# A decoder trunk on one Trainium2 core: the order and the loads of its first projections rewritten

## The chip, the core and the metric

The kernel runs on one of the eight cores of a Trainium2 chip. A core has five engines that run their own instruction queues in order and meet only at semaphores: TensorE (PE, matrix products; its weight loads are listed as PEld), VectorE (DVE), ScalarE (ACT), GpSimd (POOL) and SyncE (SP, which here issues loads). Sixteen DMA engines move data between HBM and the on-chip memory; PE writes its results to PSUM, eight banks of 128 partitions by 512 floats.

The metric is the device time of one execution in microseconds, the median of several runs. Lower is better.

## What is computed

A two-layer decoder trunk on 256 tokens of width 2048, in float32. Layer A mixes by chunked spatial gating beside cross-attention into 256 memory tokens; layer B by latent attention beside the same cross-attention; a gated feed-forward with a short convolution follows each. The change concerns what both cross-attentions need first, the keys and values of the memory, and the norm and turning of the input x:

```python
def rmsnorm(x, g):
    x32 = x.astype(jnp.float32)
    y = x32 * lax.rsqrt(jnp.mean(x32 * x32, axis=-1, keepdims=True) + EPS)
    return (y * g.astype(jnp.float32)).astype(x.dtype)

def memory_attention(q_m, mem, g_mem, w_mem_kv):
    kv = rmsnorm(mem, g_mem) @ w_mem_kv          # (256 x 2048) @ (2048 x 1024)
    k, v = kv[..., :MEM_W], kv[..., MEM_W:]      # 4 heads of 128 each
    ...
    return softmax(q k^T / sqrt(128)) v

for l in range(2):
    h = rmsnorm(x, g_mix[l])
    ...
    mo = memory_attention(q_m, mem, g_mem[l], w_mem_kv[l])
    x = x + concat(main, mo) @ w_out[l]
    x = x + conv_ffn(rmsnorm(x, g_ffn[l]), ...)
```

## The kernel before

Activations stand with features on partitions and tokens along the free axis, in blocks of 128 features: 16 blocks for a width of 2048. Every float32 operand of a product is split in two parts: a rounded high part (type fp32r) and the low part that the rounding left. An activation's two parts lie side by side as 128 x 512 (256 tokens high, 256 low); a weight tile has `whi` and `wlo`.

A projection goes in chunks of 512 KB of weights: two blocks of 128 rows by 512 columns. `chunk` (L92) loads one (L98, issued by SP, into one of five `raw` buffers), lets ACT round it to `whi` (L122, one instruction for each block, with the gain folded in) and DVE form `wlo` (L123). There are three buffers each of `whi` and `wlo`. Two kinds of projection use it:

- `gemm_fm` (L158), features out on partitions. A chunk gives eight high products of 512 columns (L140) and eight low products of 256 (L144), into four PSUM banks; `mm_fm` (L135) alternates which kind goes first from chunk to chunk (its argument `turn`).
- `gemm_tm` (L184), tokens out on partitions. A chunk gives twelve products of 512 columns (L179, L180, L181) into two banks.

Both take `hooks`: functions that are called in the code after a given chunk's products.

`start` (L417) is the beginning of the kernel. It makes keys and values of the memory for both layers: for each layer a `gemm_fm` (keys) and a `gemm_tm` (values), eight chunks each, four projections in a row. Around them it prepares inputs by hooks:

- `token_load` (L380) loads a quarter of the memory (or of x) as two pieces of 128 tokens by 512 features, 256 KB each (L383).
- `token_transpose` (L385) turns four blocks by PE transposes against the identity, four for each PSUM bank (L390), and hands the bank to `put_mem`, where ACT copies the high part (L436) and DVE forms the low part (L437) of `memhl`, or to `put_x`, where the gain is applied (L231, L232) and x is copied (L442).
- `token_rstd` (L395) sums squares by ACT (L402, eight instructions for the memory, eight for x), then a short chain on DVE and ACT gives the reciprocal root (L241 to L246; its square root L242 needs an activation table load). `spread` (L407) turns it to the feature layout by two products with ones.
- `gains` (L301) loads gain vectors (L309), turns them (L313) and stores them as columns of `gT`; the first weights' rounding needs `g_mem`.

The memory's reciprocal root scales the keys in their eviction (`ek`, L470: ACT copies, DVE adds, GpSimd multiplies by `mrb`, L471) and the values in theirs (L474). The keys are read first by `memory_scores` (L485) in layer A.

The code is a recording: a scheduler orders each engine's instructions by its own estimate of times, from their data dependencies. Within a `manual_schedule` context the listed engines keep the order of the code. Before the change no part of `start` stands in one.

## Time and profile before

| | |
|---|---|
| median of 3 runs | 2126.27 us (2125.35 to 2126.89) |
| the profiled execution | 2125.63 us |
| its span, first to last instruction | 2123.9 us |
| PE busy | 2101.8 us (99%) |
| DVE, ACT, POOL busy | 1464.5, 1147.8, 319.6 us |
| HBM read | 387.88 MB |
| granted TensorE clock over the span | 0.999 |

How to read it: one execution was recorded by the hardware profiler; times are microseconds from the span's start. Matrix products are pipelined and the ends of their records are modelled, so the records overlap and busy time is not peak use; the distance from one product's start to the next is the better measure. A timeline merges neighbouring instructions of one engine, line and operation: it gives the first start, the time to the last end, and the count; in brackets, the engine's idle time before and what ended it. A window row gives, for PE, PEld, DVE, ACT and POOL, busy time and (in brackets) instructions, then the granted clock, the share of the 16 DMA engines and GB/s. A group's row gives line, engine, operation, output and input names, shapes, count, total busy time, mean duration in ns of one, and the idle time before.

### The profile page before, as it was taken

The numbers are of one execution on the slowest core, as the hardware profiler recorded it, in microseconds if no ns is written. First come the engines' busy times: TensorE is split into PE (matmuls) and PEld (weight loads), VectorE is DVE, ScalarE is ACT, GpSimd is POOL, SyncE is SP. The second block draws the span as 40 slices with busy tenths as digits, with TensorE's granted clock in tenths as the row PEclk, the third lists the DMA queues.
The fourth block names the chain that finished last, engine by engine and source line by source line (L and its number), as shares of the span: only waits on it lengthen the run. The fifth ranks groups of instructions, "written<-read, shape, count | busy, mean of one in ns | idle before, by whom it ended". The sixth has DMA issues, their size and how long they took to land.

```text
span 2123.9 us, 31119 instructions
## 1 busy us (share of the span) xinstructions
PE 2101.8 (99%) x11624; PEld 1828.7 (86%) x11624; DVE 1464.5 (69%) x2186; ACT 1147.8 (54%) x1773; POOL 319.6 (15%) x378
## 2 busy tenths in 40 slices
PE   8999999999999999999999999999999999999998
PEld 7888888888888888888888888888888888888886
DVE  6656667777656776567788676777764677646775
ACT  7654744556435555355546555456553555535554
POOL 0000123212001110011244111221110011100110
PEclk9999999999999999999999999999999999999999
DMA  8566565666566665666555533665666666666654
GB/s 277 177 204 183 155 194 187 188 190 191 189 192 183 197 187 191 188 189 189 188 183 168 161 115 122 188 188 176 190 191 195 189 188 190 193 193 189 188 188 149
DMA packets 207548, 392.01 MB, mean 185 GB/s; under 512 B 14302, under 2 KB 22820, under 8 KB 207268
## 3 DMA queue, kind: packets, MB, share of 16 engines
q1 hardware_dynamic: 207252, 389.50, 60.4%
q8 instruction: 91, 1.49, 0.3%
q14 instruction: 61, 0.50, 0.1%
q10 hardware_dynamic: 144, 0.52, 0.1%
HBM read 387.88 MB, written 2.10 MB: 184 GB/s over the span
## 4 chain that ended last, share of the span: by engine, by line
PE 98%; DVE 1%; ACT 0%; POOL 0%; DMA 0%; issue 0%; SPq 0%; DVEq 0%; ACTq 0%
PE ps L140 51%; PE ps L144 26%; PE ps L179 6%; PE ps L181 6%; PE ps L180 6%; PE ps L829 1%; PE ps L827 0%; PE ps L520 0%; PE ps L390 0%; DMA raw<-in_w_mem_kv 0%; PE ps L485 0%; PE ps L663 0%; DVE wlo L106 0%; PE ps L850 0%; PE ps L935 0%
## 5 line engine op out<-in xcount | busy, mean ns | idle before, releaser
L118 DVE TENSOR_TENSOR wlo<-raw,whi 128x1024 fp32r<-128x1024 f32 x660 | 817.9, 1240 | 494.1 <-ACT whi L117 490.1
L117 ACT ACTIVATE whi<-raw 128x1024 fp32r<-128x1024 f32 x660 | 697.7, 1057 | 640.8 <-PE ps L140 422.2
L140 PE MATMUL ps<-xhl,whi 128*128 128x512 f32 x3280 | 789.3, 391 | 1.6 <-ACT whi L122 1.6
L140 PEld LDWEIGHTS ps<-xhl,whi 128*128 128x128 f32 x3280 | 601.5, 188 | 117.1 <-ACT whi L122 1.8
L144 PEld LDWEIGHTS ps<-xhl,wlo 128*128 128x128 f32 x3280 | 423.3, 191 | 17.9 <-DVE wlo L106 0.7
L144 PE MATMUL ps<-xhl,wlo 128*128 128x256 f32 x3280 | 432.3, 283 | 0.2 <-DVE wlo L106 0.2
L568 POOL TENSOR_TENSOR a<-js,rbc 128x256 f32<-128x256 f32 x176 | 170.1, 978 | 1164.5 <-DVE js L221 1015.2
L140 PE MATMUL ps<-h,whi 128*128 128x512 f32 x704 | 168.6, 391 | 0.0
L140 PEld LDWEIGHTS ps<-h,whi 128*128 128x128 f32 x704 | 129.3, 188 | 25.0
L571 ACT ACTIVATE c<-a,cT 128x256 f32<-128x256 f32 x176 | 100.0, 592 | 77.1 <-POOL a L568 77.1
L219 ACT ACTIVATE cr<-ps 128x256 f32<-128x256 f32 x243 | 90.6, 379 | 92.0 <-PE ps L140 82.9
L180 PE MATMUL ps<-wlo,h 128*128 128x512 f32 x352 | 136.4, 389 | 0.0
L181 PE MATMUL ps<-whi,h 128*128 128x512 f32 x352 | 136.4, 389 | 0.0
L179 PE MATMUL ps<-whi,h 128*128 128x512 f32 x352 | 123.6, 389 | 0.0
L140 PE MATMUL ps<-mainhl,whi 128*128 128x512 f32 x512 | 122.7, 391 | 0.0
L221 DVE TENSOR_TENSOR js<-ps,cr 128x256 f32<-128x256 f32 x213 | 89.5, 421 | 44.7 <-ACT cr L219 24.6
L123 DVE SCALAR_TENSOR_TENSOR wlo<-raw,gT,whi 128x512 fp32r<-128x512 f32 x112 | 87.4, 819 | 32.8 <-ACT whi L122 31.7
L140 PEld LDWEIGHTS ps<-mainhl,whi 128*128 128x128 f32 x512 | 94.1, 188 | 18.2
L573 DVE SCALAR_TENSOR_TENSOR c<-a,cT,c 128x254 f32<-128x254 f32 x176 | 102.9, 586 | 1.6
L572 DVE SCALAR_TENSOR_TENSOR c<-a,cT,c 128x255 f32<-128x255 f32 x176 | 93.3, 550 | 13.4 <-ACT c L571 12.4
L122 ACT ACTIVATE whi<-raw,gT 128x512 fp32r<-128x512 f32 x112 | 74.8, 716 | 40.4 <-PE ps L140 16.7
L144 PEld LDWEIGHTS ps<-h,wlo 128*128 128x128 f32 x704 | 90.4, 191 | 3.5
(248 smaller groups left out, 1847.0 us busy)
## 6 DMA issues: line engine op xcount, KB each, us to landing
raw<-in_w_ffn_up SPq DMA_DIRECT2D x352, 512.0 KB
raw<-in_w_ffn_down SPq DMA_DIRECT2D x176, 512.0 KB
raw<-in_w_out SPq DMA_DIRECT2D x64, 512.0 KB
raw<-in_w_in_a SPq DMA_DIRECT2D x56, 512.0 KB
raw<-in_w_mem_kv SPq DMA_DIRECT2D x32, 512.0 KB
raw<-in_w_in_b SPq DMA_DIRECT2D x16, 512.0 KB
raw<-in_w_uq SPq DMA_DIRECT2D x12, 384.0 KB
raw<-in_w_kv_a SPq DMA_DIRECT2D x8, 512.0 KB
```

What stands on the lines that cost most here:

```text
L117: nc.scalar.activation(hi[:, :n], raw[:, :n], AF.Copy)
L118: nc.vector.tensor_tensor(lo[:, :n], raw[:, :n], hi[:, :n].bitcast(F32), ALU.subtract)
L140: mm(acc[:, :], wh, x, start=first, stop=last)
L144: mm(acc[:, S:], wl, x[:, :S], start=False, stop=False)
L179: mm(acc, xh, wh, start=first, stop=False)
L180: mm(acc, xh, wl, start=False, stop=False)
L181: mm(acc, xl, wh, start=False, stop=last)
L219: self.nc.scalar.activation(cr, acc[:, S:], AF.Copy)
L568: nc.gpsimd.tensor_tensor(a, self.join(acc), rb, ALU.mult)
L571: nc.scalar.activation(c, a, AF.Identity, scale=w(2), bias=w(3))
L572: nc.vector.scalar_tensor_tensor(c[:, 1:], a[:, : S - 1], w(1), c[:, 1:], ALU.mult, ALU.add)
L573: nc.vector.scalar_tensor_tensor(c[:, 2:], a[:, : S - 2], w(0), c[:, 2:], ALU.mult, ALU.add)
```

## The change

All of it lies in the helpers named above and in `start`:

- The memory's loads are cut differently: blocks 0 to 1, 2 to 3, 4 to 7, 8 to 11, 12 to 15. The first two pieces go out on SP with `g_mem` between them. The third pair follows before the projection; the last two are hooks after chunks 1 and 3.
- The first weights' load is issued by ACT, ahead of everything else there, and given to `chunk` ready made.
- The first projection (keys, layer 0) stands in `manual_schedule` for ACT, DVE, PE and SP. Blocks 0 to 3 are turned ahead of it, blocks 4 to 15 by hooks, two blocks (one PSUM bank, four transposes) after each of the chunks 0 to 5. `mm_fm` gets turn 0 for all its chunks: high products first.
- The memory's squares move from the first projection to the value projection of layer 0 (after chunks 0 and 1), the squares of x from one hook (chunk 4 of layer 1's keys) to four (chunk 6 of layer 1's keys, chunks 0 to 2 of its values); `token_rstd` keeps the sum and the root, with one reduction in place of two. The squares are kept in the order of the code.
- The keys of layer 0 are evicted unscaled (ACT, DVE), and `scale_keys` multiplies them in place on GpSimd once `mrb` is known.
- The loads and turns of x and the constants move between hooks as shown.

```diff
-    def chunk(self, src, nk, ncol, gains=None, twice=False, heads=None):
+    def chunk(self, src, nk, ncol, gains=None, twice=False, heads=None, raw=None):
         nc, n = self.nc, nk * ncol
-        raw = self.wp.tile([P, 1024], F32, tag="raw", name=self.uid("raw"), bufs=5)
+        loaded = raw is not None
+        if not loaded:
+            raw = self.wp.tile([P, 1024], F32, tag="raw", name=self.uid("raw"), bufs=5)
...
-        nc.sync.dma_start(out=view(raw), in_=src)
+        if not loaded:
+            nc.sync.dma_start(out=view(raw), in_=src)
...
-    def gemm_fm(self, src, kbs, nblk, rhs, evict, nk=2, gain=None, hooks={}):
+    def gemm_fm(self, src, kbs, nblk, rhs, evict, nk=2, gain=None, hooks={}, raw=None):
...
-            hi, lo = self.chunk(src(kbs[c], nk), nk, nblk * P, g)
+            hi, lo = self.chunk(src(kbs[c], nk), nk, nblk * P, g, raw=raw if c == 0 else None)
...
-            self.mm_fm(jobs, (c // nk) % 2)
+            self.mm_fm(jobs, (c // nk) % 2 if raw is None else 0)
...
-    def token_load(self, src, tok, h):
-        c = slice(h * 512, (h + 1) * 512)
+    def token_load(self, src, tok, k0, k1):
+        c = slice(k0 * P, k1 * P)
...
-    def token_transpose(self, tok, h, put):
-        for k in range(4 * h, 4 * h + 4, 2):
+    def token_transpose(self, tok, k0, k1, put):
+        for k in range(k0, k1, 2):
...
+    def token_squares(self, tok, part, j, pool):
+        for tb in range(2):
+            junk = self.tmp(pool, [P, 512], "junk", 2)
+            ins = self.nc.scalar.activation(
+                junk, tok[tb][:, j * 512 : (j + 1) * 512], AF.Square, accum_out=part[:, tb, j : j + 1]
+            )
+            self.tc.keep_in_program_order(ins)
+
+    def token_rstd(self, part, pool, rt):
         sums = self.tmp(pool, [P, 2], "sums", 1)
-        for tb in range(2):
-            part = self.tmp(pool, [P, 4], "part", 2)
-            for j in range(4):
...
+        self.nc.vector.tensor_reduce(sums, part, AX.X, ALU.add)
         self.rstd(rt, sums, D, self.cp, "rt")
...
+            def scale_keys():
+                self.spread(mrb, mrt)
+                for b in range(MH):
+                    nc.gpsimd.tensor_tensor(self.kT[0][:, b, :], self.kT[0][:, b, :], mrb, ALU.mult)
+
+            raw = self.wp.tile([P, 1024], F32, tag="raw", name=self.uid("raw"), bufs=5)
+            src = self.rows(t["w_mem_kv"][0], 0, MW)(0, 2)
+            nc.scalar.dma_start(out=raw.rearrange("p (k c) -> p k c", k=2), in_=src)
+            mload(0, 2)()
             self.gains(("g_mem",))
-            self.token_transpose(mtok, 0, put_mem)
+            mload(2, 4)()
+            first = {c: [mturn(2 * c + 4, 2 * c + 6)] for c in range(6)}
+            first[1].insert(0, mload(8, 12))
+            first[3].insert(0, mload(12, 16))
             hooks = [
+                first,
                 {
-                    0: [mem_piece(1)], 2: [mem_piece(2)], 4: [mem_piece(3)],
-                    5: [lambda: self.token_rstd(mtok, st, mrt), lambda: self.gains(("g_mix", "g_ffn", "g_kv"))],
-                    6: [self.masks],
-                    7: [lambda: self.spread(mrb, mrt)],
+                    0: [lambda: self.gains(("g_mix", "g_ffn", "g_kv")), xload(0, 4), msq(0), msq(1)], 1: [xload(4, 8), msq(2), msq(3)],
+                    2: [lambda: self.token_rstd(mpart, st, mrt), xload(8, 12)], 3: [xload(12, 16), xturn(0, 4)], 4: [self.masks],
+                    5: [scale_keys], 6: [lambda: self.gains(("g_v", "g_kv_lat", "g_q_lat"))],
                 },
+                {0: [xturn(4, 8)], 2: [xturn(8, 12)], 4: [xturn(12, 16)], 6: [xsq(0)]},
                 {
-                    0: [load(0), load(1)], 1: [load(2), load(3)], 3: [trans(0)], 5: [trans(1)],
-                    6: [lambda: self.gains(("g_v", "g_kv_lat", "g_q_lat"))],
+                    0: [xsq(1)], 1: [xsq(2)], 2: [xsq(3), lambda: self.conv_consts(0)], 3: [lambda: self.token_rstd(xpart, st, self.rt)],
+                    5: [lambda: self.spread(self.rb, self.rt), lambda: self.conv_consts(1)],
                 },
-                {0: [trans(2)], 2: [trans(3)], 4: [lambda: self.token_rstd(xtok, st, self.rt)]},
-                {1: [lambda: self.spread(self.rb, self.rt)], 2: [lambda: self.conv_consts(0)], 4: [lambda: self.conv_consts(1)]},
             ]
...
                 def ek(b, acc):
-                    nc.gpsimd.tensor_tensor(kT[:, b, :], self.join(acc), mrb, ALU.mult)
+                    if l == 0:
+                        self.join(acc, kT[:, b, :])
+                    else:
+                        nc.gpsimd.tensor_tensor(kT[:, b, :], self.join(acc), mrb, ALU.mult)
...
-                self.gemm_fm(self.rows(w, 0, MW), list(range(NB)), MH, m, ek, gain=g, hooks=hooks[2 * l])
+                ET = mybir.EngineType
+                with tc.manual_schedule(engines={ET.Activation, ET.DVE, ET.PE, ET.SP}) if l == 0 else nullcontext():
+                    if l == 0:
+                        mload(4, 8)()
+                        mturn(0, 2)()
+                        mturn(2, 4)()
+                    self.gemm_fm(
+                        self.rows(w, 0, MW), list(range(NB)), MH, m, ek, gain=g, hooks=hooks[2 * l], raw=raw if l == 0 else None
+                    )
```

Here `mload`, `mturn`, `xload`, `xturn`, `msq` and `xsq` wrap `token_load`, `token_transpose` and `token_squares` for the memory and for x. Lines below the edits stand 3 to 30 further down in the changed kernel: L122 becomes line 125, L140 line 143, L144 line 147, L179 to L181 lines 182 to 184, L390 line 393, L436 line 442.

More of the change, by code (lines that the diff above doesn't have):

```diff
@@ L442, in put_x @@
                 nc.scalar.activation(self.x[:, k : k + 2, :], acc.rearrange("p (k s) -> p k s", k=2), AF.Copy)
-            def mem_piece(h):
-                return lambda: (self.token_load(t["mem"][0], mtok, h), self.token_transpose(mtok, h, put_mem))
-            load = lambda h: lambda: self.token_load(t["x"][0], xtok, h)
-            trans = lambda h: lambda: self.token_transpose(xtok, h, put_x)
-            self.token_load(t["mem"][0], mtok, 0)
+            mload = lambda k0, k1: lambda: self.token_load(t["mem"][0], mtok, k0, k1)
@@ new lines, in start @@
+            mturn = lambda k0, k1: lambda: self.token_transpose(mtok, k0, k1, put_mem)
+            xload = lambda k0, k1: lambda: self.token_load(t["x"][0], xtok, k0, k1)
+            xturn = lambda k0, k1: lambda: self.token_transpose(xtok, k0, k1, put_x)
+            mpart = st.tile([P, 2, 4], F32, name="mpart")
+            xpart = st.tile([P, 2, 4], F32, name="xpart")
+            msq = lambda j: lambda: self.token_squares(mtok, mpart, j, st)
+            xsq = lambda j: lambda: self.token_squares(xtok, xpart, j, st)
```

5 lines of the change are left out of this document (removed).

## The prediction

> **What bounds the kernel now.** First the page: span, busy time, the chain that ended last.
>
> ```profile
> span 2123.9 us, 31119 instructions
> PE 2101.8 (99%) x11624; PEld 1828.7 (86%) x11624; DVE 1464.5 (69%) x2186; ACT 1147.8 (54%) x1773; POOL 319.6 (15%) x378
> ...
> PE 98%; DVE 1%; ACT 0%; POOL 0%; DMA 0%; issue 0%; SPq 0%; DVEq 0%; ACTq 0%
> ```
>
> PE (TensorE's matrix products) is busy for 99% of the span and holds 98% of the chain, so a change counts by the time in which it makes PE stand or run slowly, and by nothing else. Such time is named by the waits of PE over the whole span (waited for, us in total, times, longest):
>
> ```profile
> PE ps L313 <- DMA graw<-in_g_mem: 5.8, 1, 5.8
> PE ps L140 <- ACT whi L122: 2.8, 2, 1.6
> PE ps L140 <- DVE qhl L232: 1.6, 1, 1.6
> ```
>
> Only the first wait, and 1.2 of the second's 2.8 us, lie in the beginning that the change rewrites. So I read the timeline of its first microseconds (start, us from the first start to the last end, engine, line, operation, count, idle before):
>
> ```profile
> 5.81 0.28 PE L313 MATMUL ps<-ident,graw 32*128 32x32 f32 x1 [5.81 <-DMA graw<-in_g_mem]
> 6.02 1.97 PE L390 MATMUL ps<-ident,mtok 128*128 128x128 f32 x8
> ...
> 7.17 0.60 ACT L436 ACTIVATE memhl<-ps 128x512 fp32r<-128x512 f32 x1 [2.91 <-PE ps L390]
> ...
> 8.40 1.33 ACT L122 ACTIVATE whi<-raw,gT 128x512 fp32r<-128x512 f32 x2 [0.63 <-DMA raw<-in_w_mem_kv]
> ...
> 9.16 1.42 DVE L123 SCALAR_TENSOR_TENSOR wlo<-raw,gT,whi 128x512 fp32r<-128x512 f32 x2 [0.66 <-ACT whi L122]
> ...
> 9.18 2.07 PE L140 MATMUL ps<-memhl,whi 128*128 128x512 f32 x4 [1.19 <-ACT whi L122]
> ...
> 11.05 1.91 PE L390 MATMUL ps<-ident,mtok 128*128 128x128 f32 x8
> ...
> 12.61 1.64 PE L140 MATMUL ps<-memhl,whi 128*128 128x512 f32 x4
> 12.65 0.57 ACT L436 ACTIVATE memhl<-ps 128x512 fp32r<-128x512 f32 x1
> ...
> 13.13 1.32 ACT L122 ACTIVATE whi<-raw,gT 128x512 fp32r<-128x512 f32 x2
> ...
> 13.50 0.68 DVE L437 TENSOR_TENSOR memhl<-ps,memhl 128x512 fp32r<-128x512 f32 x1
> ...
> 14.09 1.60 PE L144 MATMUL ps<-memhl,wlo 128*128 128x256 f32 x12
> ```
>
> and of PE alone a little later:
>
> ```profile
> 24.27 1.04 PE L390 MATMUL ps<-ident,mtok 128*128 128x128 f32 x8
> 25.07 2.11 PE L140 MATMUL ps<-memhl,whi 128*128 128x512 f32 x8
> 27.02 2.08 PE L144 MATMUL ps<-memhl,wlo 128*128 128x256 f32 x16
> 28.93 2.01 PE L140 MATMUL ps<-memhl,whi 128*128 128x512 f32 x8
> 30.78 0.23 PE L313 MATMUL ps<-ident,graw 80*128 80x80 f32 x1
> ...
> 36.93 0.39 PE L179 MATMUL ps<-whi,memhl 128*128 128x512 f32 x1
> ```
>
> The step from one row's start to the next's start, divided by the count, is the pitch. Settled: high products (L140) (30.78 - 28.93) / 8 = 0.231 us, low products (L144) (28.93 - 27.02) / 16 = 0.119, transposes (L390) (25.07 - 24.27) / 8 = 0.100. Early it is twice that: four high products from 9.18 to 11.05 (0.47 each), eight transposes from 11.05 to 12.61 (0.195); at 14.09 the low products go at (1.60 - 0.28) / 11 = 0.12. So PE runs at half speed until about 13.6 us and at full speed after (the windows' clock column, below, says 1.00 throughout; the pitch decides). From 9.18 to 36.93 are 27.75 us; the stretch holds 64 high, 64 low products, 24 transposes and five small ones: 64 x 0.231 + 64 x 0.119 + 24 x 0.100 + 0.5 = 25.3. The 2.4 us over it are the slow phase. The first projection is therefore already full after 14 us: what the change can win lies before, and what it can lose is any hole that it cuts afterwards.
>
> **The change, part by part.** PE's work itself stays: the same 32 transposes of memory, products and spreads.
>
> *The written order* is the part that decides. In the first projection PE, ACT, DVE and SP keep the order in which the code stands. Chunk c's products are followed by its hook, the four transposes of two more blocks and their copy by ACT (L436 now, line 442 after), and only then comes the chunk call for c+1, with ACT's rounding of its weights (L122 now, 125 after). The built program has it so; ACT's queue from its start:
>
> ```
> L442 Activation memhl_81<-ps_121 128x2x256
> L125 Activation whi_132<-raw_99,gT 128x512 x2
> L442 Activation memhl_81<-ps_154 128x2x256
> L125 Activation whi_162<-raw_161,gT 128x512 x2
> L442 Activation memhl_81<-ps_187 128x2x256
> L125 Activation whi_195<-raw_194,gT 128x512 x2
> ```
>
> ps_154 holds transposes that stand on PE behind the last low product of whi_132's chunk. So whi_162, which is needed next, waits on ACT behind a copy that waits for PE to finish the chunk before: PE stands while ACT copies and rounds. Before, ACT rounds the third chunk's weights at 13.13 (8.40 was the first chunk's), while PE is in the first chunk until 15. Behind the waiting copy are queued ACT's rounding of chunk c+1, behind that DVE's low part, behind both PE. It holds for chunks 1 to 6; chunk 7 has no transposes ahead of it.
>
> One such chunk, from its first transpose at t = 0, at full clock: the fourth transpose starts at 0.30 and ends 0.27 later (24.27 + 1.04 less the last start, 24.27 + 7 x 0.11). ACT follows the end of a record by about 0.05 (7.17 against 6.02 + 3 x 0.22 + 0.42 = 7.10): copy at 0.62. Its next instruction starts 0.48 later (12.65 to 13.13): rounding at 1.10. The pair takes 1.33 (8.40), so its second half, on which the second product waits, ends at 2.43, and PE goes on 0.05 later (at most 0.11: 9.18 against 8.40 + 1.33 / 2) at 2.48. Seven high products remain, 7 x 0.231, plus 0.10 for the first load of weights after another kind of work (2.11 against 2.01 for the same eight): 4.20. Eight low products, 0.95: 5.15. DVE's low part is ready earlier: its copy starts at 1.24, takes 0.68 (13.50), then 1.42 for the pair, done at 3.35. Without a hole the chunk is 4 x 0.100 + 8 x 0.231 + 8 x 0.119 = 3.20. Loss 1.95 us, six times: **11.7 us**. Bounds: ACT following without delay and the 0.10 not paid gives 1.75 (10.5); the copy's 0.60 in full ahead of the rounding (+0.12), both releases at 0.11 (+0.12) and the pair's halves without overlap (+0.1) give 2.3 (13.8). I take 1.95, which has the rows' own distances. PE work that fills such a hole later does not exist: everything behind is shifted.
>
> *The first pieces.* SP's first loads and what the DMA engines did:
>
> ```profile
> 0.81 0.86 SPq L383 DMA_DIRECT2D mtok<-in_mem  x2
> 1.72 0.42 SPq L309 DMA_DIRECT2D graw<-in_g_mem  x1
> 2.19 0.42 SPq L98 DMA_DIRECT2D raw<-in_w_mem_kv  x1
> ```
>
> ```profile
> 7.80:9.20 1.40, 0.21 (x2) 0.03 (x1) 0.73 (x2) 0.80 (x2) 0.00 (x0) 1.00 1.00 334
> 9.20:13.60 4.40, 4.40 (x14) 3.72 (x15) 3.40 (x6) 3.82 (x8) 0.00 (x0) 1.00 1.05 399
> 13.60:36.90 23.30, 23.30 (x144) 20.79 (x143) 16.10 (x35) 22.59 (x54) 0.00 (x0) 1.00 0.93 315
> ```
>
> The last two columns are the DMA engines' share and GB/s. PE's first work waits for the gains (5.81). They stood behind 512 KB of memory and stand now behind 256 KB, but the first weights (512 KB) are issued by ACT at about the same time and may be served beside them. If only SP's queue counts, the gains come 256 KB earlier, 0.8 us at the 334 GB/s of 7.80:9.20; if ACT's transfer is served first, 0.8 us later. With the gains where they are: the eight slow transposes end at 7.7 as before, two copies stand ahead of the rounding instead of one (the second at 8.05, when the eighth transpose has ended), which starts at 8.6 instead of 8.40, and the second product waits for the second half, 9.98. Seven products at 0.47 end at 13.3, the low ones (one at 0.24, seven at 0.119) at 14.4. By 15.04 (14.09 + 8 x 0.119) the kernel before has done the same and eight transposes more, worth 0.8 at full speed: 15.2 against 15.04, **+0.2 us**, with the gains' bounds -0.6 to +1.0. I take the middle, since the two orders of service lie equally far.
>
> The Trainium skill, "DMA: Bandwidth & Descriptors" (Issuing engines are not separate DMA queues), says that loads started by several engines run on the same 16 DMA engines and interleave, and that only the issue time is saved; this speaks against the move to ACT's queue, and by it the gains come late rather than early, +1.0 in place of +0.2. The trace agrees in so far as the DMA share is 1.00 and 1.05 while the first weights are under way.
>
> *Two more issues on SP* (ten pieces of memory instead of eight; 0.43 each by 0.81 0.86 x2) and the eight x pieces, 2 MB, which the built order puts ahead of the seventh weights: 2 MB take 6.7 us at the 315 GB/s of 13.60:36.90. They start behind the sixth weights, whose buffer chunk 0 gives back at about 10, and are in by about 20; the seventh weights also need chunk 1's buffer (14.4 + 3.35) and are wanted at 14.4 + 5 x 5.15 + 1.1 = 41. Nothing; the cover is those 20 us, past which each one late is one at the end.
>
> *Squares moved to the value projection and later.* There ACT now has eight roundings at 1.33, eight squares, four copies for the join, and some of the x work:
>
> ```profile
> L402 ACT ACTIVATE junk<-mtok 128x512 f32<-128x512 f32 x8 | 5.0, 620 | 2.1 <-DMA mtok<-in_mem 2.1
> L231 ACT ACTIVATE xhl<-ps,gT 128x256 fp32r<-128x256 f32 x16 | 6.8, 468 | 2.2 <-DVE xhl L232 2.2
> L442 ACT ACTIVATE xT<-ps 128x512 f32<-128x512 f32 x8 | 4.4, 587 | 0.3 <-DVE xhl L232 0.3
> L219 ACT ACTIVATE cr<-ps 128x256 f32<-128x256 f32 x8 | 2.8, 379 | 1.3 <-PE ps L140 1.0 <-DVE js L221 0.2
> L474 ACT ACTIVATE mv<-ps,mrt 128x512 f32<-128x512 f32 x4 | 2.8, 688 | 1.2 <-PE ps L181 1.2
> L242 ACT ACT_TABLE_LOAD x1 | 1.3, 1283 | 0.0
> ```
>
> 8 x 1.33 + 8 x 0.62 + 4 x 0.47 + 2 x 0.59 + 4 x 0.38 + 2 x 0.69 + 1.28 + 0.4 (sqrt, spread) = 23.2 us, less about 0.1 of overlap for each of 38: 20 to 23. PE has there 96 products of 0.23 and eight transposes, 22.9. ACT is full but not over, and enters the stage three roundings ahead (PE's holes leave it free). Value **0**; bound +1.6, the table load and the sqrt bare.
>
> *The rest*: GpSimd's scaling of the keys behind the projection instead of in its eviction is wanted only by the memory scores (L485), long after; two reductions fewer on DVE. Nothing, hidden by PE's products.
>
> **Sum.** 11.7 + 0.2 + 0 = 11.9 us on the span of 2123.9: 2135.8. The profiled execution took 2125.63, 1.7 more than its span; the median, 2126.27, lies 0.6 above that execution. So **2138.2 us** for the median, 0.56% slower. By the parts' bounds, 10.5 - 0.6 to 13.8 + 1.0 + 1.6: 2136.2 to 2142.7.
>
> **Rivals.**
> *PE falls back to half speed in the holes.* It ran at half speed until 13.6 although it had worked since 5.81, with a pause of 1.2 us in between; so pauses of about 2 us in every 5 may bring that back. A chunk then takes: transposes at 0.2, the copy at 1.1, the second half rounded at 2.9, seven products at 0.47 and eight low ones at 0.24: 8.1. Loss 4.9, six times 29.5 us: 2156. Against it the waits' third row: PE stood 1.6 us for L232, and this is how it went on:
>
> ```profile
> 1185.66 0.39 PE L181 MATMUL ps<-whi,chl 128*128 128x512 f32 x1
> 1187.64 1.67 PE L140 MATMUL ps<-qhl,whi 128*128 128x512 f32 x6 [1.58 <-DVE qhl L232]
> 1189.14 1.12 PE L144 MATMUL ps<-qhl,wlo 128*128 128x256 f32 x8
> ```
>
> From one start to the next PE did nothing new for 2.0 us, and the six products after it follow at 0.25, full speed. That is one pause, not six in a row, so the rival keeps 11%.
> The Trainium skill, "TensorE: Matmul & The Clock Gate" (Part 1), has the clock drop after an idle window of about 3.4 us, by which pauses of 2 us keep full speed; its section on psum-queue depth-cycling has frequent short pauses bring the drop. The trace agrees with the first (2.0 us, no drop); no run here shows the second.
>
> *ACT becomes the bound in the value projection.* If each of eight chunks waits for one square (0.62), 5.0 us more: 2143.2. For it: 23.2 against 22.9 and moved work that stood in an ACT with little to do. Against it: the lead of three roundings. 12%.
>
> *No hole, hence not slower.* If the rounding for c+1 were done before the copy (by two chunks' weights being in ACT's queue ahead of the transposes), only the start would remain, -0.6 to +1.0: 2125.7 to 2127.3. It decides at one point: PE's idle time in front of the second chunk's first product is under 0.3 us. For it: in the trace before ACT runs that far ahead. Against it: the built order above. 6%.
>
> **Chances.** Forecast 71%, half speed 11%, ACT 12%, no hole 6%. A measurement here tells 0.2% (4.3 us) from no change. The three slower cases all pass it except for a corner of the forecast: slower 92%, same 6%, faster 2%. The range takes the forecast's bounds, goes down a little for holes of less than their lower bound, and up past the ACT rival to a part of the half-speed case (one or two chunks at half speed, 3 us each): 2134 to 2146.5.
>
> **What would show it.** In the changed profile: PE waiting for ACT's whi (line 125) about six times, 1.2 to 1.6 us by the idle column, and for the last time before 42 us; between them 16 products and four transposes with a period near 5.15 us; the first value product (line 182) at about 46 to 48 instead of 36.93; pitches of 0.231 and 0.119 in between; from there both programs in step, so that the shift seen at the first value projection is the whole difference at the end. Wrong if the period is 3.2 (no hole), 8 (half speed), or if the shift grows by over 2 us between the first value projection and layer A.

## The result, and the profile after

The changed kernel takes 2137.45 us (median of 6 runs, 2136.90 to 2138.09), the kernel before 2126.25 beside it (6 runs): a ratio of 1.0053, 95% interval 1.0042 to 1.0063. It is slower by 11.2 us; 2138.2 was forecast. The profiled execution took 2137.39 us, its span 11.8 us more than that of before. The page's own lines:

```profile
span 2135.7 us, 31103 instructions
PE 2105.6 (99%) x11624; PEld 1829.4 (86%) x11624; DVE 1464.1 (69%) x2184; ACT 1146.9 (54%) x1773; POOL 319.5 (15%) x378
...
PE 97%; DVE 1%; ACT 1%; DMA 0%; issue 0%; SPq 0%; DVEq 0%; ACTq 0%
```

PE is busy 3.8 us longer (the eight high products of a set are recorded with 2.50 us behind a hole, as from 42.99 below, and with 2.09 without one, as in e1), and a point of the chain has gone to ACT; the rest of the 11.8 us is idle time of PE. The waits of PE over the whole span (waited for, us in total, times, longest) say for what:

```profile
PE ps L143 <- ACT whi L125: 10.7, 8, 1.6
```

The wait for ACT's `whi` went from 2.8 us in 2 times to 10.7 in 8. The longest, 1.6, lies in layer B and is in both. Before it are seven waits of 1.3: the one of the very first product, which the kernel before had too (1.19), and six new ones. One of the six, in the timeline of all engines (weight loads left out):

```profile
20.36 0.60 PE L393 MATMUL ps<-ident,mtok 128*128 128x128 f32 x4
...
20.99 0.60 ACT L442 ACTIVATE memhl<-ps 128x512 fp32r<-128x512 f32 x1 [3.35 <-PE ps L393]
21.48 1.32 ACT L125 ACTIVATE whi<-raw,gT 128x512 fp32r<-128x512 f32 x2
...
22.25 2.04 PE L143 MATMUL ps<-memhl,whi 128*128 128x512 f32 x6 [1.29 <-ACT whi L125]
```

It is the chunk of the prediction, step by step: the transposes' last start is 20.36 + 3 x 0.11 = 20.69, ACT's copy follows at 20.99, its rounding at 21.48, and PE's first high product at 22.25. It starts after the first half of the rounding; the second product waits for the second half. The last of the six and what follows it, in PE's timeline:

```profile
41.09 0.60 PE L393 MATMUL ps<-ident,mtok 128*128 128x128 f32 x4
42.99 2.50 PE L143 MATMUL ps<-memhl,whi 128*128 128x512 f32 x8 [1.29 <-ACT whi L125]
...
47.33 0.62 PE L182 MATMUL ps<-whi,memhl 128*128 128x512 f32 x2
```

From 20.36 to 41.09 there are four chunks: (41.09 - 20.36) / 4 = 5.18 us for one; 5.15 was forecast, and 3.24 is what a chunk takes without a hole (measured below). The first value product (line 182) starts at 47.33 instead of 36.93; eleven products of the last keys' chunk still stand behind it and are issued by 50.06. The windows show where PE's time was lost and where it wasn't:

```profile
14.00:45.00 31.00, 22.55 (x116) 17.44 (x116) 12.76 (x20) 12.35 (x21) 0.00 (x0) 1.00 0.60 204
...
48.00:70.00 22.00, 22.00 (x108) 18.10 (x106) 15.66 (x33) 18.41 (x41) 0.58 (x1) 1.00 0.66 210
```

In 14:45 PE has 22.55 of 31 us, and ACT, for which it waits, has 12.35: an engine that is idle 60% of the stage holds up the one that bounds it, by order alone. From 48 on PE is full, while ACT works 18.4 of 22 us beside it (in 70:92 18.6): the moved squares cost nothing.

### The profile page after: what moved, and what is told of

It is laid out like the page before. It is cut to its first block, busy times and chain, and to the rows that moved or that the text cites. A ratio compares the mean times of both kernels' runs of the same rounds, so it can differ in the third digit from the quotient of the medians.

```text
span 2135.7 us, 31103 instructions
## 1 busy us (share of the span) xinstructions
PE 2105.6 (99%) x11624; PEld 1829.4 (86%) x11624; DVE 1464.1 (69%) x2184; ACT 1146.9 (54%) x1773; POOL 319.5 (15%) x378
## 3 DMA queue, kind: packets, MB, share of 16 engines
q8 instruction: 91, 1.49, 0.3%
## 4 chain that ended last, share of the span: by engine, by line
PE 97%; DVE 1%; ACT 1%; DMA 0%; issue 0%; SPq 0%; DVEq 0%; ACTq 0%
PE ps L143 51%; PE ps L147 26%; PE ps L182 6%; PE ps L184 6%; PE ps L183 6%; PE ps L860 1%; PE ps L858 0%; PE ps L551 0%; ACT whi L125 0%; PE ps L393 0%; PE ps L516 0%; PE ps L694 0%; DVE wlo L109 0%; DMA graw<-in_g_mem 0%; PE ps L881 0%
## 5 line engine op out<-in xcount | busy, mean ns | idle before, releaser
L126 DVE SCALAR_TENSOR_TENSOR wlo<-raw,gT,whi 128x512 fp32r<-128x512 f32 x112 | 88.8, 833 | 23.6 <-ACT whi L125 22.9
L147 PE MATMUL ps<-h,wlo 128*128 128x256 f32 x704 | 91.5, 283 | 0.0
```

What stands on the lines that cost most here:

```text
L147: mm(acc[:, S:], wl, x[:, :S], start=False, stop=False)
```

## The experiments

Eleven more kernels ran. Each stands beside runs of the kernel before on the same chip, whose medians lie between 2125.80 and 2125.86 (2126.25 for the change); the table's ratios are against those.

| | median us | ratio, 95% interval |
|---|---|---|
| the change | 2137.45 | 1.0053, 1.0042 to 1.0063 |
| e1_weights_ahead | 2125.15 | 0.9996, 0.9987 to 1.0006 |
| e2_no_written_order | 2125.01 | 0.9996, 0.9986 to 1.0005 |
| e3_four_blocks_a_turn | 2132.27 | 1.0031, 1.0020 to 1.0043 |
| e4_one_more_copy | 2145.22 | 1.0096, 1.0081 to 1.0111 |
| e5_act_free | 2132.36 | 1.0030, 1.0019 to 1.0042 |
| e6_first_weights_sp | 2136.90 | 1.0051, 1.0036 to 1.0066 |
| e7_early_products | 2131.15 | 1.0024, 1.0015 to 1.0034 |
| e8_all | 2126.27 | 1.0001, 0.9993 to 1.0010 |
| e9_ten_early_products | 2124.49 | 0.9994, 0.9985 to 1.0003 |
| e10_pe_sp_order | 2124.90 | 0.9996, 0.9987 to 1.0005 |
| e11_gains_first | 2124.20 | 0.9992, 0.9984 to 1.0001 |

### Do the holes come from the written order, and are they all of it?

*e1_weights_ahead* keeps everything, the written order too, and writes chunk c+1's load, rounding and split ahead of chunk c's products and hook:

```diff
-            hi, lo = self.chunk(src(kbs[c], nk), nk, nblk * P, g, raw=raw if c == 0 else None)
+            if raw is None:
+                hi, lo = self.chunk(src(kbs[c], nk), nk, nblk * P, g)
+            else:
+                if c == 0:
+                    ahead = self.chunk(src(kbs[0], nk), nk, nblk * P, g, raw=raw)
+                hi, lo = ahead
+                if c + nk < len(kbs):
+                    ahead = self.chunk(src(kbs[c + nk], nk), nk, nblk * P, [gain(kbs[c + nk + i]) for i in range(nk)])
```

> The changed kernel with one edit: chunk c+1's weights are loaded, rounded and split ahead of chunk c's products and hook, still in written order. Theory (ACT's rounding stands behind a copy that waits for PE): the six holes go, PE waits for whi once, at the first chunk; 2125.9 us (2125 to 2127), that is about 0.6 for the first two copies and the later clock, less about 1.0 that the changed kernel gains in layer B. Rival (the cost lies in the smaller pieces of memory, in the load order or in PE's fixed order): still above 2130.

*e2_no_written_order* lets the scheduler order the first projection:

```diff
-                with tc.manual_schedule(engines={ET.Activation, ET.DVE, ET.PE, ET.SP}) if l == 0 else nullcontext():
+                with nullcontext():
```

> The changed kernel without the written order, all else kept; ACT's rounding then stands up to three chunks ahead of the copies. Theory: no regular hole, 2125.9 us (2125 to 2127.5). Rival (moved squares and loads cost something of their own): 2130 or more.

2125.15 and 2125.01: both give back the whole loss. Each against the runs beside it, the change is 11.2 us slower than the kernel before, e1 0.7 and e2 0.8 faster: 11.9 and 12.0 between them, 2.0 for each of six holes. PE's timeline of e1, with its own line numbers (ACT's copy is L449 there):

```profile
18.47 2.09 PE L143 MATMUL ps<-memhl,whi 128*128 128x512 f32 x8
...
21.71 2.09 PE L143 MATMUL ps<-memhl,whi 128*128 128x512 f32 x8
```

No idle column, and 3.24 us from one chunk's first product to the next's. ACT's copy still stands in front of a rounding and still waits for PE's transposes, but the rounding behind it is now the one for the chunk after next:

```profile
18.75 0.60 ACT L449 ACTIVATE memhl<-ps 128x512 fp32r<-128x512 f32 x1 [1.42 <-PE ps L400]
19.24 1.33 ACT L125 ACTIVATE whi<-raw,gT 128x512 fp32r<-128x512 f32 x2
```

The rounding of 19.24 has a whole chunk of PE (18.47 to 21.71) to hide behind. The hole is a matter of what stands behind the copy, and not of the copy.

*e3_four_blocks_a_turn* keeps the change's order but turns four blocks after every second chunk, so that roundings stand behind a turn three times instead of six:

```diff
-            first = {c: [mturn(2 * c + 4, 2 * c + 6)] for c in range(6)}
-            first[1].insert(0, mload(8, 12))
-            first[3].insert(0, mload(12, 16))
+            first = {c: [mturn(2 * c + 4, 2 * c + 8)] for c in (0, 2, 4)}
+            first[1] = [mload(8, 12)]
+            first[3] = [mload(12, 16)]
```

> The changed kernel with four blocks turned after each of chunks 0, 2 and 4 instead of two after each of chunks 0 to 5; written order kept. Theory (a hole for each turn, not for each chunk): three holes of about 2.0 us (copy of the second bank, rounding, restart), so 6 us less than the changed kernel, but layer B's gain of 1.0 is not there in this build: 2132.5 us (2131.5 to 2133.5). Rival (cost for each chunk, from written order on PE or from high products always first): 2137 to 2138.

2132.27 us, as expected. PE's timeline has holes behind every second chunk only:

```profile
22.84 1.04 PE L393 MATMUL ps<-ident,mtok 128*128 128x128 f32 x8
25.22 2.50 PE L143 MATMUL ps<-memhl,whi 128*128 128x512 f32 x8 [1.34 <-ACT whi L125]
...
28.49 2.00 PE L143 MATMUL ps<-memhl,whi 128*128 128x512 f32 x8
...
31.29 1.03 PE L393 MATMUL ps<-ident,mtok 128*128 128x128 f32 x8
```

The chunk that begins at 28.49 has no idle column: no turn stands in front of it. From 22.84 to 31.29 are 8.45 us for eight transposes and two chunks' products, which take 8 x 0.100 + 16 x 0.231 + 16 x 0.119 = 6.40 at full pitch: 2.05 for a hole. The price goes by the number of turns, not of blocks.

### Whose order is it?

*e5_act_free* takes ACT out of the written order; PE, DVE and SP keep it:

```diff
-tc.manual_schedule(engines={ET.Activation, ET.DVE, ET.PE, ET.SP})
+tc.manual_schedule(engines={ET.DVE, ET.PE, ET.SP})
```

> The changed kernel with ACT alone taken out of the written order; PE, DVE and SP keep it. Theory (ACT's order alone cuts the holes): 2125.9 us (2125 to 2127.5), PE's order as in the changed kernel and no regular wait. Rival (PE's or DVE's written order shares in it): 2129 to 2136.

2132.36: the theory that ACT's queue alone is to blame fell. The waits for `whi` are gone from the beginning, and others have taken their place; first the row of PE's waits, then ACT and DVE in the timeline, around PE's transposes of 24.85 and the fourth chunk's high products, which start at 25.20:

```profile
PE ps L147 <- DVE wlo L126: 4.3, 9, 2.2
```

```profile
13.56 2.79 ACT L125 ACTIVATE whi<-raw,gT 128x512 fp32r<-128x512 f32 x4 [1.45 <-DMA raw<-in_w_mem_kv]
...
24.03 1.34 ACT L125 ACTIVATE whi<-raw,gT 128x512 fp32r<-128x512 f32 x2 [2.21 <-DMA xtok<-in_x]
...
25.48 0.60 ACT L442 ACTIVATE memhl<-ps 128x512 fp32r<-128x512 f32 x1
...
26.11 0.69 DVE L443 TENSOR_TENSOR memhl<-ps,memhl 128x512 fp32r<-128x512 f32 x1 [2.26 <-ACT memhl L442]
26.72 1.41 DVE L126 SCALAR_TENSOR_TENSOR wlo<-raw,gT,whi 128x512 fp32r<-128x512 f32 x2
```

ACT now rounds far ahead: the four instructions of 13.56 are the third and the fourth chunk's, done by 16.35, and the row of 24.03 is the sixth chunk's. (That one needs the buffer of the third: it starts 0.18 behind the end of the third chunk's low part, as the next one does behind the fourth's.) ACT's copy comes 0.63 behind the first of the transposes, 24.85 to 25.48, as in the changed kernel, 20.36 to 20.99. But DVE's written order has the low part of the activations (L443) ahead of the low part of the fourth chunk's weights (L126). The latter could have been formed any time after 16.35, and starts at 26.72, behind a copy that waits for PE. It is the same hole, now on DVE. PE's low products stand for it. A chunk takes 4.27 us (PE's transposes at 24.85, 29.12, 33.39), 1.03 over e1's 3.24. The first such hole is longer, 2.22 us before 18.26, and behind it the clock was at half from 19.50 to 22.91; both are in the 6.5 us that e5 loses to the kernel before.

*e10_pe_sp_order* frees DVE as well:

```diff
-tc.manual_schedule(engines={ET.Activation, ET.DVE, ET.PE, ET.SP})
+tc.manual_schedule(engines={ET.PE, ET.SP})
```

> Only PE and SP keep the written order in the first projection; ACT and DVE are ordered by the scheduler. Theory (ACT's copies ahead of the rounding and DVE's low parts of the activation ahead of the low parts of the weights cut the holes, PE's own order is harmless): no hole, period 3.2, 2125.1 (2124.5 to 2126), as without any written order. Rival (PE's order alone leaves a hole, since the scheduler can't move its products): 2129 to 2133.

2124.90. One hole of 0.54 us is left in the stage, at the third chunk; the next chunks follow each other by 3.23 (transposes at 20.77, 24.00, 27.24):

```profile
17.87 2.11 PE L143 MATMUL ps<-memhl,whi 128*128 128x512 f32 x8 [0.54 <-DVE memhl L443]
```

So the written order of PE costs nothing that can be told, and DVE's cuts holes even with ACT free. (e10's profiled execution took 2126.50, 1.6 over its median; the clock was at half for one stretch of it, in layer B, of which more below.) To lose nothing, both had to be freed, or (e1) both given the next weights in time. ACT kept with DVE free wasn't tried; that ACT's order cuts holes is read from the changed kernel, where PE waits for `whi` and DVE's part follows in time.

### How near was half speed?

*e4_one_more_copy* makes each of the six holes longer by one 128 x 512 copy on ACT between the turn and the rounding (of memory that is there already, read by nobody):

```diff
+            more = lambda: nc.scalar.activation(self.tmp(st, [P, 512], "junk", 2), mtok[0][:, 0:512], AF.Copy)
+            for c in range(6):
+                first[c].append(more)
```

> The changed kernel with one more ACT copy of 128x512 (read by nobody) behind each of the six turns, that is between memhl's copy and the rounding. Theory (ACT's queue from transposes to rounding is the path): each hole grows by one start-to-start of such a copy, 0.5 us, six times: 2140.4 us (2140 to 2141.2). Rival (PE waits for something else, ACT's copy is beside the path): 2137.5, no change.

2145.22, 4.8 us over the expectation, 7.8 over the change. The added wait itself was as expected: 1.81 in place of 1.29 ahead of each first product, 0.52 for each hole, 3.1 for six. Four chunks are 1.4 to 1.6 us longer than that, 6.0 together, of which 1.3 is given back at the start, where the full clock came at 12.81 instead of 15.57. The four are longer in the products' own durations:

```profile
16.29 2.50 PE L143 MATMUL ps<-memhl,whi 128*128 128x512 f32 x8 [1.81 <-ACT whi L125]
...
29.23 3.96 PE L143 MATMUL ps<-memhl,whi 128*128 128x512 f32 x8 [1.81 <-ACT whi L125]
```

Four of the six sets of eight high products (at 21.99, 29.23, 36.50 and 49.27) take 3.6 to 4.0 us instead of 2.5: half speed for a part of each. The windows are cut at the trace's clock records, which follow each other by 3.41 us (columns: PE busy and instructions, then PEld, DVE, ACT, POOL; granted clock; share of the DMA engines; GB/s):

```profile
12.81:16.23 3.42, 1.67 (x13) 1.39 (x12) 0.69 (x1) 1.72 (x4) 0.00 (x0) 1.00 1.05 395
...
23.05:26.47 3.42, 3.42 (x13) 2.84 (x12) 0.34 (x1) 0.00 (x0) 0.00 (x0) 0.50 0.76 245
...
33.29:36.71 3.42, 1.61 (x13) 1.34 (x12) 0.92 (x2) 1.99 (x4) 0.00 (x0) 1.00 0.13 47
40.12:43.53 3.41, 1.63 (x13) 1.35 (x12) 0.69 (x1) 1.75 (x4) 0.00 (x0) 1.00 0.22 85
```

Four stretches were followed by one at half clock (23.05:26.47 is one of these): those from 19.64, 26.47, 33.29 and 46.95, in which PE was busy for 1.48, 1.49, 1.61 and 1.49 us. Those from 12.81 and 40.12, with 1.67 and 1.63, were not. In the changed kernel such stretches have 2.0 to 2.1 (15.57:18.99, 18.99:22.40, 25.81:29.23: 2.02, 2.12, 2.01). The half-speed rival of the prediction was half a microsecond of pause away. One of e4's four executions took 2148.88, 3.6 to 3.8 over the others; no trace of it was kept.

### The start

*e6_first_weights_sp* issues the first weights on SP behind the gains, as everything else:

```diff
-            nc.scalar.dma_start(out=raw.rearrange("p (k c) -> p k c", k=2), in_=src)
             mload(0, 2)()
             self.gains(("g_mem",))
+            nc.sync.dma_start(out=raw.rearrange("p (k c) -> p k c", k=2), in_=src)
             mload(2, 4)()
```

> The changed kernel with the first weights issued by SP, behind the first memory pieces and the gains, instead of by ACT. Theory (the queue matters little, as the rounding starts when ACT has made its second copy): first work between 5.0 and 5.9 us, first product 8.5 to 9.4, 2137.2 us (2136.5 to 2138). Rival (ACT's queue brings the first weights in time and SP's does not): first product after 10 us, 2138.5 or more.

2136.90, no difference to the change that can be told. The time was as expected, the places weren't: first work at 3.90 (5.0 to 5.9 was said), first product at 9.81 (8.5 to 9.4):

```profile
3.90 0.28 PE L316 MATMUL ps<-ident,graw 32*128 32x32 f32 x1 [3.90 <-DMA graw<-in_g_mem]
...
7.24 1.27 PE L393 MATMUL ps<-ident,mtok 128*128 128x128 f32 x4 [2.02 <-DMA mtok<-in_mem]
...
9.81 3.97 PE L143 MATMUL ps<-memhl,whi 128*128 128x512 f32 x8 [1.29 <-ACT whi L125]
```

Without 512 KB from ACT's queue beside them the gains are in at 3.90 us; with them it was 5.86. The Trainium skill, "DMA: Bandwidth & Descriptors" (Issuing engines are not separate DMA queues), says that loads issued by several engines share the same 16 engines and interleave; the two numbers agree. The two microseconds don't last: the second four transposes wait 2.02 us for memory pieces that now stand behind the weights, and the first product starts at 9.81 (9.34 in the change).

Four kernels tried to win something at the start. *e7_early_products* adds 18 float32 products of the identity with ones, read by nobody, ahead of all other work of PE in the kernel before; *e8_all* adds them to e1, with the gains' load ahead of the first memory pieces; *e9_ten_early_products* is e8 with eight of them (`range(8)`, not the ten of its label); *e11_gains_first* has none.

```diff
+            acc = self.psum()
+            for _ in range(18):
+                nc.tensor.matmul(acc[:, :P], self.ones, self.ident, start=True, stop=True)
...
-            mload(0, 2)()
             self.gains(("g_mem",))
+            mload(0, 2)()
```

> The kernel before with 18 products of the identity with ones (read by nobody) at the head of PE's queue, while it waits for the gains. Theory (the slow phase ends a few us after PE begins to work, and costs 2 us behind the first product): full speed from 7 us at the latest, first product still at 9.2 as the weights land at 8.3, 2124.7 us (2124 to 2125.9). Rival (the slow phase is hidden by the wait for the next weights, released by their loads at 11.4): 2126.2, no change.

> The changed kernel with chunk c+1's weights ahead, the same 18 early products, and the gains' load ahead of the memory's pieces. Theory: no hole, no slow phase, gains in about 1 us earlier; first product near 8 us and all of it at full speed: 2123 us (2121.8 to 2124.5). Rival (the first product waits for the memory's pieces or the first weights as before): 2124.5 to 2126.

> As e1_weights_ahead (each chunk's load, rounding and split written ahead of the chunk before), with the gains' load first on SP and eight early products of the identity with ones (read by nobody) ahead of everything on PE; with 18 of them the records showed 36, the last from 8.27 us, and the gains' turn came at 8.30. Theory (the clock needs PE busy for about 5 us from 1.67 on, and 18 products only held up the gains): eight give 16 records, done at about 5.0 us, the gains are turned by 5.9, the first product starts by 9.3 at full speed, so against e1 the slow stretch's 2.9 us go: 2122 to 2123.5, the layer B wait for kr deciding 1.0 of it. Rival (the early work is too short, the clock comes on at 10 or later): 2124 to 2125.5. Rival (memory pieces behind the gains come late): first product after 10.5, 2125 or more.

> As e1_weights_ahead, with the gains' load first on SP, ahead of the first memory pieces, and no early products. If the gains hold PE up at the start (5.77 in e1), the first PE work comes earlier but the transposes wait for the memory pieces, which arrive 0 to 0.4 us later: 2124.8 to 2125.6, no difference to e1 that can be told. If the 128 KB ahead of the memory count in full, up to 2126.

e7, e8 and e9 missed the theory's number, and e11 lies under its range. PE's timeline shows most of why; first of e7, then of e8, e9 and e11:

```profile
14.39 3.78 PE L140 MATMUL ps<-memhl,whi 128*128 128x512 f32 x8 [5.10 <-DVE memhl L437]
```

```profile
8.30 0.24 PE L323 MATMUL ps<-ident,graw 32*128 32x32 f32 x1
...
10.91 2.49 PE L143 MATMUL ps<-memhl,whi 128*128 128x512 f32 x8 [1.35 <-ACT whi L125]
```

```profile
5.78 1.65 PE L400 MATMUL ps<-ident,mtok 128*128 128x128 f32 x8 [0.44 <-DMA mtok<-in_mem]
8.72 3.54 PE L143 MATMUL ps<-memhl,whi 128*128 128x512 f32 x7 [1.29 <-ACT whi L125]
```

```profile
2.55 0.28 PE L323 MATMUL ps<-ident,graw 32*128 32x32 f32 x1 [2.55 <-POOL swap L298]
...
8.85 3.54 PE L143 MATMUL ps<-memhl,whi 128*128 128x512 f32 x7 [1.29 <-ACT whi L125]
```

- 18 float32 products are 36 records (16 for eight), two for each, and last to about 8.1 us in e7: the gains, in by 5.8, wait for PE until 8.02. In e7 PE also waits 5.10 us for DVE's low part ahead of the first product (14.39, before: 9.18): the scheduler laid ACT's work out anew, a square and two chunks' roundings (9.26 to 12.80) ahead of a copy whose transposes had ended at 9.29. The clock, full from 6.17, was at half again from 13.00 to 19.82. 2131.15 instead of 2124.7.
- e8 has the full clock from 6.75 on, seven microseconds earlier than the kernel before, and yet no gain: gains at 8.30, first product at 10.91, 1.66 later than e1's 9.25. From the second turn on it is 0.5 to 0.7 us ahead of e1, from the value projection on 0.2, and it loses 1.0 in layer B (below). 2126.27 instead of 2123.
- e9 ends its early work in time (gains turned at 5.09, first product 8.72), but loses the clock again: full from 4.73, half from 8.14 to 14.97. This is an execution of 2126.04, 1.5 over the median; whether the others lost the clock too isn't shown. The median is 2124.49 where 2122 to 2123.5 was expected (the rival had 2124 to 2125.5), and the fastest of eleven 2123.04; the wait for `kr` in layer B (below), which it has and e1 has not, costs it 1.0.
- e11 turns the gains at 2.55 and has the first product at 8.85, half a microsecond before the change and 0.4 before e1. 2124.20, a little under its expected 2124.8 to 2125.6. It is the fastest that ran, 1.6 us under the kernel before; its interval ends at 1.0001, so that it is faster isn't established.

## Why the prediction was right

*The written order, 11.7 us.* Right in mechanism, place, number and size. Measured: period 5.18 for 5.15, six waits of 1.29 to 1.30, the last from 41.70 to 42.99 (before 42 was said). That the first value product, at 47.33, lies in the 46 to 48 that was said is luck: the sum itself puts it at 36.93 + 11.9 = 48.8, and it came early because eleven products of the keys were left for behind it. Against e1, which has the same start, the same products are 0.10 us later at the second set of transposes (14.81 against 14.71) and 11.97 at the first value product (47.33 against 35.36): 11.9 us for six holes, 1.98 each where 1.95 was predicted. By the medians, each against the runs beside it, it is 11.9 as well.

What the prediction named as the cause was too narrow. It put the hole on ACT's queue, with DVE's low part "ready earlier". e5 shows that DVE's order cuts a hole of 1.0 where ACT has rounded in time; in the change the wait for ACT hides it, and it isn't free.

*The first pieces, +0.2 us (-0.6 to +1.0).* The gains came where they were before (5.86 against 5.81), which was the value taken; e6 shows that it was a balance and not the absence of an effect: half the memory ahead of them is worth 1.9 us (5.81 to 3.90; 0.8 was estimated), and ACT's load beside them takes 2.0 back (3.90 to 5.86). In the profiled executions the start cost more: the shift from one kernel to the other, after the holes, is 12.7 us (1160.03 to 1172.74 for the same set of products in the fences below), 0.8 over the holes' 11.9 (e1, which has no holes, stands 0.66 behind the kernel before at that set). The term was mis-sized on that reading, within its bounds; the working let the full clock come at 13.6 us as before, and it came at 15.57. That is no property of the change: among the kernels that share its start the clock records turn to full at 15.57, 15.04 (e1), 13.99 (e3) and 12.81 (e4), always a whole number of 3.41 us from any other switch of the same execution and without relation to the start of the kernel. The Trainium skill, "TensorE: Matmul & The Clock Gate" (What's actually happening), calls the window free-running, so that the moment varies from run to run; the trace agrees. The start's price can therefore not be told from a single execution to better than a microsecond.

*What the prediction hadn't: 1.0 us given back in layer B.* It expected both programs in step from the first value product on. They are from about 105 us on, when the moved work is done in both, for a thousand more, and then the changed kernel gains one: the wait of PE for `kr` (L748 on L765 before) is gone. GpSimd and PE there, before:

```profile
1160.03 3.82 PE L140 MATMUL ps<-xhl,whi 128*128 128x512 f32 x16
...
1163.15 1.18 POOL L261 TENSOR_TENSOR qls<-qls,sq 128x256 f32<-128x256 f32 x1
...
1164.29 1.18 POOL L765 TENSOR_TENSOR kr<-js,rbc 128x256 f32<-128x256 f32 x1
...
1165.53 0.70 PE L748 MATMUL ps<-kr,swap 128*128 128x256 f32 x2 [0.73 <-POOL kr L765]
...
1167.02 0.86 PE L140 MATMUL ps<-xhl,whi 128*128 128x512 f32 x3
```

and after:

```profile
1172.74 3.82 PE L143 MATMUL ps<-xhl,whi 128*128 128x512 f32 x16
...
1175.87 1.18 POOL L796 TENSOR_TENSOR kr<-js,rbc 128x256 f32<-128x256 f32 x1
...
1177.71 0.60 PE L779 MATMUL ps<-kr,swap 128*128 128x256 f32 x2
...
1178.74 1.54 PE L143 MATMUL ps<-xhl,whi 128*128 128x512 f32 x6
```

In the first, GpSimd makes a sum `qls` (1163.15) ahead of `kr` (1164.29), and PE, whose next instruction turns `kr`, stands 0.73 us. In the second `kr` comes first and PE finds it ready. The shift goes from 12.71 (1172.74 - 1160.03) to 11.72 (1178.74 - 1167.02). No line of the diff touches this place: the scheduler laid the same instructions out otherwise. PE waits for `kr` 0.7 us in e3, e7, e8 and e9 as well, not in the other seven; e9, which is 0.32 us ahead of e1 until there, is 0.67 behind it afterwards. Which of the two layouts comes out follows no part of the edits that I could name, and it is worth a microsecond either way. So the span came out right (2135.8 for 2135.7) by small errors that cancel, which is luck: 0.2 too little for the holes, 0.6 too little for the start, 1.0 not seen in layer B. The 0.7 between 2138.2 and 2137.45 is another: the forecast added the 0.6 by which the profiled execution of before lies under its median, and that of the change lies 0.06 under its own.

*ACT in the value projection, 0, with a rival of 12%.* Right: PE is full in 48:70 and 70:92. The step "ACT is full but not over" overstated ACT: 18.4 of 22 us. (Its own working, 23.2 less 0.1 for each of 38, gives 19.4 and not 20 to 23.)

*Half speed, 11%.* It didn't happen in the change, and the reason given, a single pause of 2.0 us with no drop, was too little evidence. e4 shows the rival alive with pauses of 1.81 by the idle column, and e10's profiled execution shows a drop after a single one of 1.60, in layer B:

```profile
1152.38:1155.80 3.42, 1.77 (x7) 1.20 (x8) 3.42 (x8) 3.42 (x10) 3.19 (x5) 1.00 0.00 1
```

PE waits there 1.60 us for `whi` (and 0.23 once more), a wait that the kernel before and the change have too (the "longest, 1.6" of their rows), and the next stretch has half clock. In the kernel before the same wait left 1.81 busy in its stretch (1150.25:1153.66), and the clock stayed. So a pause like the one that the prediction relied on may or may not bring the drop, by where it lies in the 3.41-us stretches. The prediction set two statements of the Trainium skill, "TensorE: Matmul & The Clock Gate", against each other, a drop after an idle window (Part 1) and one by frequent short pauses (A second HAM failure mode: psum-queue depth-cycling). The trace of e4 agrees with the second: PE was never idle for a window, only for a little over half of one. That of e10 differs from both, with one pause of under half a window, and the measurement decides.

*No hole, 6%.* Excluded by the trace: 1.29 us idle where under 0.3 was the criterion. e1 is that rival built: 2125.15, under the 2125.7 to 2127.3 where it was put, and inside without the 1.0 that it gains in layer B.

*The seventh weights and the x pieces, 0.* Right: SP issues the seventh weights at 21.63, and no row shows PE or ACT waiting for a load in 14:45.

## What to carry to other kernels

When an order is written out by hand, follow each engine's queue and ask of every instruction that waits for PE what stands behind it and when PE will want that: preparation of the next chunk must stand ahead of anything that ends with the present one, on every engine that has a part in it. Freeing or mending one engine may only uncover the next, so price each engine's order by itself. And judge small terms (a microsecond here) only after looking at places that the edit doesn't touch: the scheduler's layout and the clock's phase move them too.

## What the runs showed of the hardware

- The clock falls without any long pause. In e4 it fell after each 3.41-us stretch in which PE was busy for 1.61 us or less and stayed after 1.63 or more, came back one stretch later, and fell again at the next hole but not at every one: which hole costs 1.5 us more is decided by where it lies in the grid. The busy time is not the whole rule: in e10 the clock fell after 1.77 (1152.38:1155.80), and with the last products of the kernel it stayed after 1.64 in the change (2125.01:2128.42) and after 1.54 in e7 (2119.02:2122.44).
- Coming up asks for more than staying up. In all thirteen traces the full clock came behind a stretch in which PE was busy for 3.06 us or more, and 2.84 or less never brought it. In e9, in stretches of 3.41 us:

```profile
1.32:4.73 3.41, 3.06 (x14) 3.06 (x15) 0.52 (x2) 1.25 (x1) 1.14 (x5) 1.00 0.70 230
4.73:8.14 3.41, 2.14 (x13) 1.27 (x11) 0.93 (x3) 1.27 (x3) 0.00 (x0) 1.00 0.97 318
8.14:11.56 3.42, 2.84 (x6) 2.12 (x7) 2.12 (x4) 2.04 (x4) 0.00 (x0) 0.50 0.97 296
11.56:14.97 3.41, 3.41 (x16) 3.14 (x14) 1.27 (x2) 0.43 (x1) 0.00 (x0) 0.50 1.04 366
```

Before its first record, at 4.73, the column shows 1.00 for want of one. 3.06 busy of 3.41 brought full speed, 2.84 (third row) didn't bring it back, 3.41 (fourth) did. But the second row lost it with 2.14 busy, more than what e4 keeps it with. Of its 13 instructions eight are transposes (5.78, 1.65 us). The Trainium skill, "TensorE: Matmul & The Clock Gate" (Part 4: PE-mode transpose), says that transposes don't count as PE work in the same way; by that the row has about 0.5 us, and it fits. For coming up they must have counted, if busy time is the measure: in the kernel before, eight transposes take 1.56 us (11.05 to 12.61) of the stretch that brought the full clock at 13.61, and without them it has 1.85, less than what failed in e9. Whether they count for staying up no run here separates.

```profile
10.20:13.61 3.41, 3.41 (x14) 2.92 (x12) 2.42 (x5) 2.83 (x7) 0.00 (x0) 1.00 1.05 399
```

- A float32 product shows as two records, and 36 of them last 6.4 to 6.7 us. The transposes of this kernel, float32 too, show as one.
- 512 KB issued from another queue at the same moment held a small load up for two microseconds: gains at 5.86 with them, 3.90 without, with the same 256 KB of memory ahead of them on SP.
